# The first projection: rows of both operands 64 bytes apart mod 128, and two rows walked together

## The chip, the cores and the metric

The kernel runs on one core of one Trainium2 chip. The metric is device time in microseconds of one execution. The kernel before took 1110.11 us, the median of three runs (1110.0 to 1111.09). The profile is of one further execution, which took 1111.0 us, 1109.2 of them between its first and its last instruction.

## The reference, cut to what matters

One layer of a decoder for 256 tokens and 16 meta tokens, 2,048 wide. A normed input goes through the first projection, `w_in`, to 12,288 columns: queries, keys and values of 8 differential and 8 stick-breaking heads. Attention, the output projection and a squared-ReLU MLP follow.

```python
h = jnp.concatenate([dummy, meta, x], axis=1)
u = _rmsnorm(h, g_mix[l])
proj = jnp.einsum('bld,de->ble', u, w_in[l])          # the first projection
dq, dk, dv, sq, sk, sv = jnp.split(proj, split_at, axis=-1)
...                                                   # two kinds of attention -> mixed
h = h + jnp.einsum('ble,ed->bld', mixed, w_out[l])
m = _rmsnorm(h, g_mlp[l])
hid = jnp.square(jax.nn.relu(jnp.einsum('bld,df->blf', m, w_up[l])))
h = h + jnp.einsum('blf,fd->bld', hid, w_down[l])
```

## The kernel before

All large products are made of parts. A 32-bit operand is split into hi, its value rounded to the format in which TensorE (PE) takes it, and lo, the rest. Each product is then three matmuls into one sum: hi by hi, hi by lo, lo by hi.

The contraction over 2,048 is cut into 16 rows k of 128. For the first projection the moving operand is `u`: for each k one row of 272 tokens' hi and, right behind it, 272 tokens' lo (split_u, L165 to L171). A row is `ROW` = 576 floats long, 2,304 bytes, of which 2 x 272 are used. The stationary operand are the weights. They come in tiles of four rows k by 256 columns: the DMA brings one into `raw`, ScalarE (ACT) rounds it to `whi` (L175), VectorE (DVE) takes the difference, `wlo` (L177). A tile's four rows lie one behind the other, 1,024 bytes each. The first six tiles are split in two halves (rows 0 and 1, then 2 and 3), the later ones in one piece.

The stage has 24 strips of 256 columns, six kinds by four pairs of heads. Kinds 0 and 3, the queries, need the 256 tokens alone: their matmuls have 256 columns and begin 16 floats further in a row of `u`. The other four kinds have 272. A strip takes four weight tiles (c = 0 to 3), and each tile serves two halves j of 128 output columns, each summed in its own bank of PSUM. So a tile makes 2 x 4 x 3 = 24 matmuls, each with its own load of 128 by 128 weights (PEld in the profile). They are called in the loop over `units` behind `begin`: for each j, for each row kk of the tile, the three products (`products`, L966 to L978). L975 is hi by hi, L976 hi by lo, L977 lo by hi.

Where a weight tile's hi and lo begin is chosen in `offsets` (L244): each buffer is 64 floats longer than its data, and the data begin 0, 16 or 32 floats into it, that is 0 or 64 bytes mod 128. In the first projection lo is always 16 floats further than hi. The tiles for the output projection and the MLP take 0 or 16 for both. For the MLP's up products (L1060) it is 16 for the first tile of the first and third unit of a round, and 0 for the others.

The buffers of a kind are each 4,352 bytes long, 34 times 128, so they all begin at the same place mod 128. In the built program that is 32, and `u` begins at 96; `m`, the MLP's input, takes the same buffer as `u` later.

The order on each engine is written out by a planner (`Pace`): it keeps a model of the time on PE, DVE and ACT. The main loop issues the products; after each row it lets the planner issue whatever its model says is due: splits, loads, and the pieces of attention, whose matmuls fall between the products of the projection. `pc.stall` holds the model, not the chip, until the weights and the row of `u` are modelled as ready. The chip waits on semaphores. PE runs its queue in order.

Of the kernel before, what the change touches and what calls it, by code (L numbers as in the profile page):

```python
# [8 lines left out]
F32R = mybir.dt.float32r  # L9
# [4 lines left out]
P = 128  # L14
DM = 2048
SEQ = 256
META = 16
TOK = META + SEQ
KT = DM // P
EPS = 1e-6  # L20
NEG = -1e30
ROW = 576
LINE = 16
ROUNDS = 8
PAIRS = 4
# [97 lines left out]
def hymba_layer(ctx: ExitStack, tc: tile.TileContext, xT_d, xh_d, win_d, wout_d, wup_d, wdn_d, cst_d, par_d, out_d):  # L123
    nc = tc.nc
    cp = ctx.enter_context(tc.tile_pool(name="const", bufs=1))
    big = ctx.enter_context(tc.tile_pool(name="big", bufs=1))
# [8 lines left out]
    pc = Pace((("fetch", 9), ("weights", 9), ("once", 2), ("evac", 6), ("head", 4)))  # L135
# [23 lines left out]
    ident = cp.tile([P, P], F32, name="ident")  # L159
    xT = big.tile([P, KT, TOK], F32, tag="x", name="xT")  # L160
    big.tile([P, LINE], F32, name="pad_act")
    um = big.tile([P, KT, ROW], F32R, tag="act", name="u")[:, :, : 2 * TOK].rearrange("p k (a n) -> p k a n", a=2)
    big.tile([P, 3 * LINE], F32, name="pad_mix")
    mixed = big.tile([P, KT, 2, SEQ], F32R, tag="mix", name="mixed")

# [15 lines left out]
    strips = []  # L181
# [9 lines left out]
    order = [("in", *u) for u in dict.fromkeys(u[:2] for u in units)]  # L191
# [10 lines left out]
    for r in range(ROUNDS - 1):  # L202
        c = iter([key for i in range(PAIRS) for key in up(r + 1, i, range(4))])
# [37 lines left out]

    ring = {g: g - PARTS for g in range(len(order))}

    def offsets(g):  # L244

        what, *at = order[g]
        if what == "in":
            line = strips[at[0]][1] in (0, 3)
            return line * LINE, line * LINE + LINE
        line = at[1:] in ([0, 0], [2, 0]) if what == "up" else at != [0, 0] if what == "out" else True
        return line * LINE, line * LINE

    def part(g, pieces=1):
        if g < len(order) and g not in parts:
            pool, bufs, tag = wp, PARTS, "w"  # L260
            if g >= first_mlp:
                ring[g] = max(g - MLP_PARTS, first_mlp - PARTS + (g - first_mlp) % MLP_PARTS) if (g - first_mlp) % MLP_PARTS < PARTS else g - MLP_PARTS
                if (g - first_mlp) % MLP_PARTS >= PARTS:
                    pool, bufs, tag = mp, MLP_PARTS - PARTS, "v"
                    ring[g] = ring[g] if g - MLP_PARTS >= first_mlp else -1
            hi, lo = (
                pool.tile([P, 1024 + 4 * LINE], F32R, tag=tag + x, bufs=bufs, name=f"w{x}_{g}")[:, n : n + 1024]
                .rearrange("p (k n) -> p k n", k=4)
                for x, n in zip(("hi", "lo"), offsets(g))
            )  # L270
            parts[g] = (hi, lo)
            what, *at = order[g]
            fast = what in "ab" and (at[0], at[1]) in FAST
            pc.job("weights", (fast_a if what == "a" else fast_b)(g, hi, lo) if fast else halves(g, hi, lo, pieces))
# [46 lines left out]
    g = 0  # L321
    for c in range(4):
        n = 2 if c == 0 else 4
# [639 lines left out]
    def strip_start(s):  # L963
        return banks("acc", 2, f"acc_{s}")

    def products(s, out, j, k, kk, hi, lo):  # L966
        what, a, b = strips[s]
        cols = slice(P * j, P * j + P)
        h, l = hi[:, kk, cols], lo[:, kk, cols]
        first, last = k == 0, k == KT - 1  # L970
        if True:
            f, n = (META, SEQ) if a in (0, 3) else (0, TOK)
            xh, xl = um[:, k, 0, f : f + n], um[:, k, 1, f : f + n]
            o = out[j][:, :n]
            nc.tensor.matmul(o, lhsT=h, rhs=xh, start=first, stop=False)  # L975
            nc.tensor.matmul(o, lhsT=h, rhs=xl, start=False, stop=False)  # L976
            nc.tensor.matmul(o, lhsT=l, rhs=xh, start=False, stop=last)  # L977
            return pc.T(3 * (n / 2.4 + 2.5))  # L978
    seen_kinds = set()

    def finish(s, j, o, t):
        what, a, b = strips[s]
        if True:
            kind = "ds"[a // 3]
            gen = (diff_q, diff_k, None, stick_q, stick_k, None)[a]
            pc.job("evac", delayed(t, gen(b, j, o) if gen else values(kind, b, j, o)))
            seen_kinds.add((a, b, j))
            if a % 3 < 2 and {(a // 3 * 3, b, j), (a // 3 * 3 + 1, b, j)} <= seen_kinds:
                pc.job("head", (diff_head, stick_head)[a // 3](b, j))
# [43 lines left out]
    for s, c, kks in units:  # L1033
        g = index["in", s, c]
        if c == 0 and kks[0] == 0:
            open_strips[s] = strip_start(s)
        out = open_strips[s]
        if g >= seen:
            seen = g + 1
            begin(g, LEAD)  # L1040
        hi, lo = parts[g]
        for j in range(2):
            for kk in kks:
                k = 4 * c + kk
                pc.stall(("w", g, kk), ("u", k))
                t = products(s, out, j, k, kk, hi, lo)
                if k == KT - 1:
                    finish(s, j, out[j], t)
                pc.pump()
        if kks[-1] == 3:  # L1050
            done_at[g] = pc.pe

# [19 lines left out]
    for g in range(index["out", 0, 0], first_mlp):  # L1072
        _, u, c = order[g]
        if c == 0:
            out = banks("acc", 2, f"out_{u}")
            if u == 0:
                m = big.tile([P, KT, ROW], F32R, tag="act", name="m")[:, :, : 2 * SEQ].rearrange("p k (a n) -> p k a n", a=2)
        if u == 1 and c == 0:
            while pc.lanes["head"][0] or any(("mixed", k) not in pc.at for k in range(KT)):
                pc.pe += 100  # L1080
# [129 lines left out]
```

## Time and profile before

| what | before |
|---|---|
| median of three runs | 1110.11 us |
| the profiled execution | 1111.0 us |
| its span | 1109.2 us |
| PE busy | 1100.9 us, 99% |
| DVE busy | 945.1 us, 85% |
| ACT busy | 795.9 us, 72% |
| DMA read | 206.49 MB, 188 GB/s with the writes |
| granted PE clock | 1.00 |

An engine's busy time is the time in which at least one of its instructions runs. The matmuls of PE are pipelined: one is shown as some 280 ns long, and the next starts 110 to 130 ns behind it. So the length of a single row says little of PE's pace, and the sum of rows would be over 100%. The pace is the distance between starts, called a step here; it is read from the timeline, whose starts are given to 0.01 us, over many steps.

### The profile page before, as it was taken

How to read it: one execution, taken by the hardware profiler on the slowest of the kernel's cores; microseconds unless marked ns; L12 is line 12 of the kernel's file. 1: busy time of each engine (PE TensorE's matmuls, PEld its weight loads, DVE VectorE, ACT ScalarE, POOL GpSimd, SP SyncE). 2: the span in 40 equal slices, each digit the busy share in tenths (PEclk: the TensorE clock that was granted, in tenths of full speed). 3: DMA queues.
4: the chain of work that ended last, by engine and by line, in shares of the span. 5: the costliest groups of instructions: out<-in, count | busy, mean ns of one | idle time of the engine just before them, and what ended most of it. 6: DMA issues, size and time to landing. Idle time of an engine off the chain costs nothing.

```text
span 1109.2 us, 21822 instructions
## 1 busy us (share of the span) xinstructions
PE 1100.9 (99%) x8599; PEld 1057.5 (95%) x8599; DVE 945.1 (85%) x1459; ACT 795.9 (72%) x1283; POOL 1.1 (0%) x8
## 2 busy tenths in 40 slices
PE   8999999999999999999999999999999999999998
PEld 7999999999998888999999999999999999999987
DVE  6988988888877556689989989989989989989997
ACT  7878878878777555656677777777777677777663
POOL 0000000000000000000000000000000000000000
PEclk9999999999999999999999999999999999999999
DMA  8664544554544556545655655655655665655653
GB/s 326 188 228 144 158 135 138 169 158 143 166 159 149 191 179 221 189 154 191 227 191 191 225 192 192 224 194 191 222 192 195 219 196 193 219 194 196 213 183 137
DMA packets 58134, 210.00 MB, mean 189 GB/s; under 512 B 6576, under 2 KB 6832, under 8 KB 57904
## 3 DMA queue, kind: packets, MB, share of 16 engines
q1 hardware_dynamic: 58032, 208.61, 57.2%
q8 instruction: 67, 1.10, 0.4%
q14 instruction: 35, 0.29, 0.1%
HBM read 206.49 MB, written 2.10 MB: 188 GB/s over the span
## 4 chain that ended last, share of the span: by engine, by line
PE 98%; DVE 1%; DMA 1%; ACT 0%; SPq 0%; issue 0%; DVEq 0%
PE up L1060 32%; PE down L1066 28%; PE acc L975 9%; PE acc L977 8%; PE acc L976 8%; PE out L1066 8%; PE s_d L625 1%; DMA raw<-in_win 1%; PE po_s L665 1%; PE po_d L665 1%; PE z_s L625 1%; DVE wlo L177 0%; PE pt L829 0%; PE pq_dq L553 0%; SPq L228 0%; DVE H L899 0%
## 5 line engine op out<-in xcount | busy, mean ns | idle before, releaser
L177 DVE TENSOR_TENSOR wlo<-raw,whi 128x1024 fp32r<-128x1024 f32 (+2 forms) x478 | 538.8, 1158 | 104.0 <-ACT whi L175 102.5
L175 ACT CAST whi<-raw 128x1024 fp32r<-128x1024 f32 (+2 forms) x478 | 464.7, 997 | 200.6 <-PE up L1060 53.0
L1060 PE MATMUL up<-m,whi 128*128 128x256 f32 x2048 | 356.7, 277 | 0.0
L1066 PE MATMUL down<-whi,hid 128*128 128x256 f32 (+1 forms) x1552 | 313.1, 300 | 1.2 <-ACT down L927 1.2
L1060 PEld LDWEIGHTS up<-m,whi 128*128 128x128 f32 x2048 | 311.4, 188 | 1.9
L1060 PE MATMUL up<-m,wlo 128*128 128x256 f32 x1024 | 284.0, 277 | 0.0
L1066 PEld LDWEIGHTS down<-whi,hid 128*128 128x128 f32 x1552 | 244.1, 188 | 13.0 <-ACT down L927 1.4
L1066 PE MATMUL down<-wlo,hid 128*128 128x256 f32 (+1 forms) x776 | 233.3, 301 | 0.0
L975 PE MATMUL acc<-u,whi 128*128 128x272 f32 (+1 forms) x768 | 222.6, 290 | 1.2 <-ACT whi L175 1.2
L977 PE MATMUL acc<-u,wlo 128*128 128x272 f32 (+1 forms) x768 | 219.4, 286 | 0.7 <-DVE wlo L177 0.7
L976 PE MATMUL acc<-u,whi 128*128 128x272 f32 (+1 forms) x768 | 217.5, 283 | 0.0
L1060 PEld LDWEIGHTS up<-m,wlo 128*128 128x128 f32 x1024 | 192.8, 188 | 0.0
L1066 PEld LDWEIGHTS down<-wlo,hid 128*128 128x128 f32 x776 | 145.7, 188 | 6.3
L975 PEld LDWEIGHTS acc<-u,whi 128*128 128x128 f32 x768 | 144.5, 188 | 3.1 <-ACT whi L175 2.1
L977 PEld LDWEIGHTS acc<-u,wlo 128*128 128x128 f32 x768 | 144.3, 188 | 1.6 <-DVE wlo L177 1.5
L976 PEld LDWEIGHTS acc<-u,whi 128*128 128x128 f32 x768 | 144.5, 188 | 0.0
L1066 PE MATMUL out<-whi,mixed 128*128 128x512 f32 x256 | 80.3, 395 | 0.0
L290 DVE TENSOR_TENSOR raw<-raw 128x512 f32<-128x512 f32 x88 | 60.9, 692 | 3.0
L1066 PEld LDWEIGHTS out<-whi,mixed 128*128 128x128 f32 x256 | 47.3, 188 | 9.4
L1066 PE MATMUL out<-wlo,mixed 128*128 128x512 f32 x128 | 50.2, 392 | 0.0
L922 ACT COPY z<-down 128x512 f32<-128x512 f32 (+1 forms) x88 | 45.8, 528 | 2.9 <-PE down L1066 2.8
L871 ACT ACTIVATE hx<-up 128x512 f32<-128x512 f32 x32 | 19.1, 597 | 39.3 <-PE up L1060 39.3
(241 smaller groups left out, 918.5 us busy)
## 6 DMA issues: line engine op xcount, KB each, us to landing
raw<-in_wup SPq DMA_DIRECT2D x128, 512.0 KB, 4.7
raw<-in_wdn SPq DMA_DIRECT2D x128, 512.0 KB, 3.9
raw<-in_win SPq DMA_DIRECT2D x95, 512.0 KB, 3.7
raw<-in_wout SPq DMA_DIRECT2D x32, 512.0 KB, 3.5
H<-in_xh SPq DMA_DIRECT2D x1, 2048.0 KB, 8.4
out<-H SPq DMA_DIRECT2D x8, 256.0 KB, 2.0
xT<-in_x SPq DMA_DIRECT2D x3, 544.0 KB, 9.7
cst<-in_cst SPq DMA_DIRECT2D x1, 609.0 KB, 11.8
```

What stands on the lines that cost most here:

```text
L175: nc.scalar.copy(hi, src)
L177: nc.vector.tensor_tensor(lo, src, as32(hi), op=ALU.subtract)
L290: nc.vector.tensor_tensor(raw[:, 3::-3], first, raw[:, 3:1:-1], op=ALU.add)
L625: nc.tensor.matmul(dst, lhsT=q[x][rows, cols], rhs=k[y][rows, :n], start=i == 0, stop=i == 2)
L665: nc.tensor.matmul(o, lhsT=l, rhs=r, start=i == 0, stop=i == len(todo) - 1)
L871: nc.scalar.activation(x[:, 0:4].rearrange("p a b -> p (a b)"), o, AF.Relu)
L922: nc.scalar.copy(Z[u][:, at], o[i][:, :n])
L975: nc.tensor.matmul(o, lhsT=h, rhs=xh, start=first, stop=False)
L976: nc.tensor.matmul(o, lhsT=h, rhs=xl, start=False, stop=False)
L977: nc.tensor.matmul(o, lhsT=l, rhs=xh, start=False, stop=last)
L1060: nc.tensor.matmul(out, lhsT=w[a], rhs=x[:, b], start=first and i == 0, stop=last and i == 2, skip_group_check=True)
L1066: nc.tensor.matmul(out, lhsT=x[a], rhs=w[b], start=first and i == 0, stop=last and i == 2, skip_group_check=check)
```

## The change

The row of `u` grows from 576 to 592 floats. Its two halves, hi and lo, are now 296 floats each instead of 272, so hi begins at 0 and lo 1,184 bytes further, and neighbouring rows k are 2,368 bytes apart: 64 mod 128. A first-projection weight tile uses its whole buffer: four rows of 272 floats, of which the last 256 hold data, so neighbouring rows are 1,088 bytes apart, 64 mod 128 as well. Hi and lo begin alike. `m` keeps its place but packs its rows without a gap.

The walk changes too. For kinds of 272 columns two neighbouring rows are taken together: hi by hi of both, hi by lo of both, lo by hi of both. For kinds of 256 columns a row's three products stay together, but a tile is walked by even rows for j = 0 and 1, and then by odd rows for j = 1 and 0. The planner is let in after two rows instead of one. All products are now called from one line, L976.

```diff
-ROW = 576
+ROW = 592
...
-    um = big.tile([P, KT, ROW], F32R, tag="act", name="u")[:, :, : 2 * TOK].rearrange("p k (a n) -> p k a n", a=2)
+    um = big.tile([P, KT, ROW], F32R, tag="act", name="u").rearrange("p k (a n) -> p k a n", a=2)
...
-            hi, lo = (
-                pool.tile([P, 1024 + 4 * LINE], F32R, tag=tag + x, bufs=bufs, name=f"w{x}_{g}")[:, n : n + 1024]
-                .rearrange("p (k n) -> p k n", k=4)
-                for x, n in zip(("hi", "lo"), offsets(g))
-            )
+            whole = [pool.tile([P, 1024 + 4 * LINE], F32R, tag=tag + x, bufs=bufs, name=f"w{x}_{g}") for x in ("hi", "lo")]
+            if order[g][0] == "in":
+                hi, lo = (x.rearrange("p (k n) -> p k n", k=4)[:, :, LINE:] for x in whole)
+            else:
+                n = offset(g)
+                hi, lo = (x[:, n : n + 1024].rearrange("p (k n) -> p k n", k=4) for x in whole)
...
+        f, n = (META, SEQ) if a in (0, 3) else (0, TOK)
+        todo = [(kk, i) for i in range(3) for kk in kks] if n == TOK else [(kk, i) for kk in kks for i in range(3)]
+        for kk, i in todo:
+            k = 4 * c + kk
+            nc.tensor.matmul(
+                out[j][:, :n], lhsT=(hi, hi, lo)[i][:, kk, cols], rhs=um[:, k, i % 2, f : f + n],
+                start=k == 0 and i == 0, stop=k == KT - 1 and i == 2,
+            )
...
-        for j in range(2):
-            for kk in kks:
-                k = 4 * c + kk
-                pc.stall(("w", g, kk), ("u", k))
-                t = products(s, out, j, k, kk, hi, lo)
-                if k == KT - 1:
-                    finish(s, j, out[j], t)
-                pc.pump()
+        if strips[s][1] in (0, 3):
+            todo = [(j, [kk for kk in kks if kk % 2 == odd]) for odd in range(2) for j in (range(2), (1, 0))[odd]]
+        else:
+            todo = [(j, kks[n : n + 2]) for j in range(2) for n in range(0, len(kks), 2)]
+        for j, some in todo:
+            pc.stall(*[("w", g, kk) for kk in some], *[("u", 4 * c + kk) for kk in some])
+            t = products(s, out, c, j, some, hi, lo)
+            if 4 * c + some[-1] == KT - 1:
+                finish(s, j, out[j], t)
+            pc.pump()
...
-                m = big.tile([P, KT, ROW], F32R, tag="act", name="m")[:, :, : 2 * SEQ].rearrange("p k (a n) -> p k a n", a=2)
+                m = big.tile([P, KT * ROW], F32R, tag="act", name="m")[:, : KT * 2 * SEQ].rearrange("p (k a n) -> p k a n", k=KT, a=2)
```

On PE, in a strip of 272 columns, the last row of a weight tile and the first of the next stand like this before (`acc` is the sum in PSUM, one for each output half, `whi` and `wlo` the weights, and u the moving operand; each row is one matmul):

```order
L975 MATMUL acc_1_1919<-u,whi_1808 128x272
L976 MATMUL acc_1_1919<-u,whi_1808 128x272
L977 MATMUL acc_1_1919<-u,wlo_1809 128x272
L975 MATMUL acc_0_1918<-u,whi_1852 128x272
L976 MATMUL acc_0_1918<-u,whi_1852 128x272
L977 MATMUL acc_0_1918<-u,wlo_1853 128x272
```

The same engine in the changed program, also in a strip of 272 columns: the last two rows of a tile for the one output half, the last two for the other, and the attention scores (`z`) behind them (x4 are four matmuls of one text: hi by hi of two rows, then hi by lo of both):

```order
L976 MATMUL acc_0_3526<-u,whi_3438 128x272 x4
L976 MATMUL acc_0_3526<-u,wlo_3439 128x272 x2
L976 MATMUL acc_1_3527<-u,whi_3438 128x272 x4
L976 MATMUL acc_1_3527<-u,wlo_3439 128x272 x2
L623 MATMUL z_s_3559<-kh_s_3382,qh_s_3519 128x144
L623 MATMUL z_s_3559<-kl_s_3383,qh_s_3519 128x144
```

The three products of a row no longer stand together: six matmuls of two rows do, and neighbouring matmuls have weights of different rows.

On PE, in a strip of 256 columns, the last row of one output half and the first of the other stand like this before:

```order
L975 MATMUL acc_0_2153<-u,whi_2114 128x256
L976 MATMUL acc_0_2153<-u,whi_2114 128x256
L977 MATMUL acc_0_2153<-u,wlo_2115 128x256
L975 MATMUL acc_1_2154<-u,whi_2114 128x256
L976 MATMUL acc_1_2154<-u,whi_2114 128x256
L977 MATMUL acc_1_2154<-u,wlo_2115 128x256
```

In the changed program this is the end of one weight tile of such a strip and the start of the next, with the two matmuls of a head's norm (`pn`) between them:

```order
L976 MATMUL acc_0_2110<-u,whi_2051 128x256 x2
L976 MATMUL acc_0_2110<-u,wlo_2052 128x256
L358 MATMUL pn_s_2210<-oh_s_2163,ones 128x256
L359 MATMUL pn_s_2210<-ol_s_2164,ones 128x256
L976 MATMUL acc_0_2110<-u,whi_2112 128x256 x2
L976 MATMUL acc_0_2110<-u,wlo_2113 128x256
```

A row's three products still stand together, but the tile ends with the output half with which it began, and the next begins with that half again, so the pieces of attention fall between other rows. Before the last product of the stage PE had 439 matmuls of attention in 81 places; now it has 432 in 78.

## Rows read from the trace of the kernel before

**Rows 1.** the page: span, busy time by engine, the chain that ended last
```profile
span 1109.2 us, 21822 instructions
...
PE 1100.9 (99%) x8599; PEld 1057.5 (95%) x8599; DVE 945.1 (85%) x1459; ACT 795.9 (72%) x1283; POOL 1.1 (0%) x8
...
PE 98%; DVE 1%; DMA 1%; ACT 0%; SPq 0%; issue 0%; DVEq 0%
PE up L1060 32%; PE down L1066 28%; PE acc L975 9%; PE acc L977 8%; PE acc L976 8%; PE out L1066 8%; PE s_d L625 1%; DMA raw<-in_win 1%; PE po_s L665 1%; PE po_d L665 1%; PE z_s L625 1%; DVE wlo L177 0%; PE pt L829 0%; PE pq_dq L553 0%; SPq L228 0%; DVE H L899 0%
```

**Rows 2.** stretch: length, busy us of PE, PEld, DVE, ACT, POOL, clock, DMA
```profile
120.00:160.00 40.00, 40.00 (x336) 39.05 (x336) 36.49 (x84) 31.71 (x78) 0.00 (x0) 1.00 0.51 157
...
sum 280.00, PE 279.88 PEld 277.00 DVE 241.61 ACT 226.14 POOL 0.00; mean PE 39.98 PEld 39.57 DVE 34.52 ACT 32.31 POOL 0.00
```

**Rows 3.** PE groups, 5.5 to 338.3 us: count | busy us, mean ns | idle us
```profile
L975 PE MATMUL acc<-u,whi 128*128 128x272 f32 x512 | 149.9, 293 | 0.0
...
L975 PE MATMUL acc<-u,whi 128*128 128x256 f32 x256 | 72.6, 284 | 1.2 <-ACT whi L175 1.2
L977 PE MATMUL acc<-u,wlo 128*128 128x256 f32 x256 | 72.2, 282 | 0.7 <-DVE wlo L177 0.7
```

**Rows 4.** timeline, PE: start us, us, engine, line, operands, shape; 272 columns
```profile
165.35 0.29 PE L975 MATMUL acc<-u,whi 128*128 128x272 f32 x1
165.47 0.28 PE L976 MATMUL acc<-u,whi 128*128 128x272 f32 x1
...
172.01 0.29 PE L975 MATMUL acc<-u,whi 128*128 128x272 f32 x1
```

**Rows 5.** timeline, PE, a run of 256 columns
```profile
187.89 0.28 PE L976 MATMUL acc<-u,whi 128*128 128x256 f32 x1
...
193.66 0.28 PE L977 MATMUL acc<-u,wlo 128*128 128x256 f32 x1
```

**Rows 6.** timeline, PE, the MLP's up products (x2: two starts, one row)
```profile
455.51 0.40 PE L1060 MATMUL up<-m,whi 128*128 128x256 f32 x2
...
457.67 0.40 PE L1060 MATMUL up<-m,whi 128*128 128x256 f32 x2
...
458.03 0.39 PE L1060 MATMUL up<-m,whi 128*128 128x256 f32 x2
...
459.05 0.39 PE L1060 MATMUL up<-m,whi 128*128 128x256 f32 x2
```

**Rows 7.** groups by line and shape, DVE and ACT, splits into hi and lo
```profile
L177 DVE TENSOR_TENSOR wlo<-raw,whi 128x1024 fp32r<-128x1024 f32 x378 | 452.0, 1221 | 101.0 <-ACT whi L175 99.8 <-PE down L1066 0.3
...
L891 DVE TENSOR_TENSOR hid<-hx,hid 128x1024 fp32r<-128x1024 f32 x32 | 39.0, 1219 | 0.3 <-ACT hid L889 0.2
...
L175 ACT CAST whi<-raw 128x1024 fp32r<-128x1024 f32 x378 | 388.5, 1048 | 182.8 <-PE up L1060 50.4 <-PE down L1066 37.3 <-DVE raw L294 36.5
...
L889 ACT CAST hid<-hx 128x1024 fp32r<-128x1024 f32 x32 | 33.5, 1048 | 2.7 <-DVE hx L883 2.7
```

**Rows 8.** timeline, PE, the start, with waits in brackets
```profile
5.59 0.39 PE L975 MATMUL acc<-u,whi 128*128 128x256 f32 x1 [0.83 <-ACT whi L175]
...
6.32 0.39 PE L977 MATMUL acc<-u,wlo 128*128 128x256 f32 x1 [0.22 <-DVE wlo L177]
...
8.18 0.38 PE L975 MATMUL acc<-u,whi 128*128 128x256 f32 x1 [0.41 <-ACT whi L175]
```

**Rows 9.** timeline, PE, up products around four transposes
```profile
436.35 0.39 PE L1060 MATMUL up<-m,whi 128*128 128x256 f32 x2
...
438.05 0.39 PE L1060 MATMUL up<-m,whi 128*128 128x256 f32 x2
...
438.74 0.60 PE L829 MATMUL pt<-ident,H 128*128 128x128 f32 x4
...
439.53 0.40 PE L1060 MATMUL up<-m,whi 128*128 128x256 f32 x2
...
441.30 0.40 PE L1060 MATMUL up<-m,whi 128*128 128x256 f32 x2
```

More of the change, by code (lines that the diff above doesn't have):

```diff
@@ L242, in hymba_layer, with offset @@
     ring = {g: g - PARTS for g in range(len(order))}
-    def offsets(g):
+    def offset(g):
         what, *at = order[g]
-        if what == "in":
-            line = strips[at[0]][1] in (0, 3)
-            return line * LINE, line * LINE + LINE
         line = at[1:] in ([0, 0], [2, 0]) if what == "up" else at != [0, 0] if what == "out" else True
-        return line * LINE, line * LINE
+        return line * LINE
     def part(g, pieces=1):
@@ L964, in strip_start, with products @@
         return banks("acc", 2, f"acc_{s}")
-    def products(s, out, j, k, kk, hi, lo):
+    def products(s, out, c, j, kks, hi, lo):
         what, a, b = strips[s]
         cols = slice(P * j, P * j + P)
[L969 to L978, printed above, removed]
+        f, n = (META, SEQ) if a in (0, 3) else (0, TOK)
[6 more added lines that the diff above has]
+            )
+        return pc.T(3 * len(kks) * (n / 2.4 + 2.5))
     seen_kinds = set()
```

## The prediction

> **What bounds the kernel now.** I read the page first. TensorE (PE) is busy 99% of the span, VectorE (DVE) 85%, ScalarE (ACT) 72%, and the chain of waits that ended last is 98% PE; 25% of it is the three product lines of the first projection, L975 to L977 [rows 1]. So the change works on the engine that sets the end, and a nanosecond saved per product there is a nanosecond of the span unless another engine becomes late. Next the stretches: from 40 to 320 us PE idles 0.12 us of 280, at the full granted clock (1.00, the 2.4 GHz level), while DVE is busy 241.61 us, or 86%, with 36.49 of 40 in the tightest stretch [rows 2]. There is nothing to win from waits, only from the step between the starts of two neighbouring products. The groups by shape give the counts: three lines of 512 products with 272 columns, three of 256 with 256 columns, so 1,536 and 768 [rows 3]; their only waits are 1.2 and 0.7 us, all at the start.
>
> The busy times of a group overlap (a product is shown as 0.29 us long, the next starts 0.12 us behind it [rows 4]), so I take steps from the timeline. 272 columns: starts at 165.35 and 172.01, 54 steps apart, 123.3 ns each [rows 4]. 256 columns: 187.89 to 193.66, 49 steps, 117.8 ns [rows 5]. The same 256 columns in the MLP's up products: 455.51 to 457.67, 18 steps of 120.0 ns, and right behind it 458.03 to 459.05, 9 steps of 113.3 ns [rows 6]. Same engine, clock, shape and kind of operand: three levels, 113, 118 and 120.
>
> What differs between the last two is the weights' place. In the built program the moving operand of the up products begins 96 bytes into a 128-byte line in both; the stationary one begins at 96 in the slow group (`line` is 1 for that weight tile) and at 32 in the other. Both operands are read by PE at once: the load of the next weights goes on while the present product streams. So 64 bytes apart is good, the same half line costs 6.7 ns a step.
>
> The Trainium skill, "TensorE: Matmul & The Clock Gate", section "Step-by-step: what each phase is for", says the opposite: the two operands come through independent read ports, and loading the next weights takes no read bandwidth from the running product. By that rule places would not matter and the sum would be zero; the trace disagrees, with 120.0 against 113.3 ns.
>
> **What the first projection does now.** Worked out from the layout, (stationary, moving) bytes mod 128 run, for 272 columns, (32, 96), (32, 32), (96, 96), over and over, and the 256-column kinds have the same with every number moved by 64. The next weights are always 64 away from the present stream, as in the good up group. But the stream jumps: a 272-column row is 1,088 bytes, so it ends 64 further than it began; (32, 96) runs on seamlessly into (32, 32), that one into (96, 96), and then the third breaks. With 256 columns two of the three steps break. So I read 123.3 and 117.8 as a good level plus breaks. The good level for 256 columns is 113.3; for 272 I scale it by columns, 113.3 x 272/256 = 120.4. The poor level for 272 is likewise 117.8 x 272/256 = 125.2.
>
> **The change part by part.** It adds and removes no product: 2,304 before and after.
>
> 1. 272 columns (16 of the 24 strips). Two rows are walked together, hi-hi, hi-lo, lo-hi: (96, 96), (32, 32), (96, 0), (32, 64), (96, 96), (32, 32). The hi-lo rows stand 32 off, since a half of a 592-float row is 1,184 bytes, 32 mod 128. Three of the six steps (inside hi-hi, inside lo-hi, and on to the next pair) are now seamless with the next weights 64 away: 120.4. The other three touch a hi-lo product: into it the stream jumps by 32, inside it the next weights are 32 away, out of it both. No row of before shows operands 32 apart in this stage; the bounds are the good and the same-half level, 120.4 and 120.0 x 272/256 = 127.5. I take the middle between the good and the poor level, 122.8, since 32 is half of the 64 that a break has now. Mean (120.4 + 122.8)/2 = 121.6, a gain of 1.7 ns x 1,536 = 2.6 us (bounds: 2.9 x 1,536 = 4.5 us, and with 127.5 for the three a mean of 124.0, a loss of 1.0 us).
>
> 2. 256 columns (8 strips). Even rows first for both halves, then odd rows, so the stationary place stays, and the moving one runs 32, 64, 32, with the weights at 96 (odd rows: 64 further). One step in three is exactly like the good up group, 113.3. The two that touch the shifted row lie between 113.3 and 120.0; by the same choice I take 115.6, the middle between 113.3 and 117.8. Mean 114.8, gain 3.0 x 768 = 2.3 us (bounds 4.5 x 768 = 3.5 us, and none, with 120.0 for the two).
>
> 3. The splitting into hi and lo writes four pieces of 256 with gaps instead of one run of 1,024 for these 96 weight tiles. Cost nothing: hid is written in gapped pieces of 128 already, and takes 1,219 ns on DVE against 1,221 in one run, 1,048 against 1,048 on ACT [rows 7].
>
> 4. The wider row moves all later tiles by 1,024 bytes, a multiple of 128, and m packs its rows 2,048 instead of 2,304 bytes apart, also multiples; the output and MLP products keep their places mod 128. Cost nothing, save that a level can be inherited (below).
>
> 5. Start-up. The even-odd walk asks for rows 2 and 3 of a weight tile after three products instead of six. In the first 12 us PE already waits for splits 0.83, 0.22 and 0.41 us [rows 8], and tiles arrive in two halves there. I add 0.2 us, with 0 and 1.5 us (four such tiles by 0.4) as ends: what waits earlier there waits less later, since the same loads and splits end the chain.
>
> 6. Cover. PE would be through with the stage some 5 us sooner in 330, 1.5%; DVE at 86% goes to 87.5%, and its tightest stretch from 91 to 93%. I cost this at nothing; if that cover were gone, ACT's and DVE's queue of attention pieces would make PE wait, and what is won is the most that could be lost.
>
> Sum: 2.6 + 2.3 - 0.2 = 4.7 us. The profiled execution took 1111.0 us (span 1109.2 and 1.8 around it), so 1106.3; the median of the runs is 0.9 below that execution, so 1105.4.
>
> **Rivals.**
> - All steps go to the good level, because a 32-byte jump breaks nothing: 2.9 x 1,536 + 4.5 x 768 = 4.5 + 3.5, less 0.2, 7.8 us: 1102.3. For it: up products hold 113.3 over long runs. Against: nothing shows a 32-byte offset to be free.
> - The level is inherited, not set by places. After four transposes at 438.74 the up products, same line, same shape, same places, go from 113.3 (436.35 to 438.05, 15 steps) to 118.0 (439.53 to 441.30, 15 steps) [rows 9], and stay there until the 120 ns group; behind that they are at 113.3 again [rows 6]. The first projection is cut by attention products some 80 times, so each piece may draw either level whatever the walk is: (120.4 + 125.2)/2 = 122.8 and (113.3 + 117.8)/2 = 115.6 would still gain 0.8 + 1.7 = 2.5 us, all poor levels would lose 1.9 x 1,536 = 2.9 us, and a mix of them nothing. I put this case at 1110, from 1108 to 1112.
> - The other side: the hi-lo products collide, and the stream comes out of it at the poor level. Three of six 272-column steps at 127.5 and the others at 125.2 give 126.4, a loss of 3.1 x 1,536 = 4.8 us; two of three 256-column steps at 120.0 and one at 117.8 give 119.3, a loss of 1.5 x 768 = 1.2 us; with the start's 0.2, 6.2 us: 1116.3. It decides once the three steps behind a collision don't recover; if they do, the loss is 1.0 + 0.2 and the time 1111.3. For it: same-half reads cost 6.7 ns without fail, and now even the seamless step in three of the 256-column kinds leaves the mean at 117.8. Against: 32 apart is not the same place, and behind the 120 ns group the stream recovered at once [rows 6].
>
> - Places don't matter in this stage: the 123.3 and 117.8 come from something else in it, such as the splits' traffic, and stay. The start's 0.2 us alone is left: 1110.3. Against it speak the 6.7 ns between the up groups, where the same kind of split runs beside the products [rows 6]. This is the time by the Trainium skill's rule of independent ports, quoted above.
>
> **How the numbers follow.** Forecast 0.37, all good 0.21, inherited 0.21, collision 0.16, no effect of places 0.05. A measurement of this kernel can tell about 0.2% (2.2 us) from no change, so faster means under 1107.9 and slower over 1112.3. Faster: most of the first two and a little of the third, 0.58; same: most of the third, the last, the forecast's weak end and the collision that recovers, 0.28; slower: the collision that doesn't, and the start's 1.5 us on top of no gain, 0.14. The range runs from all good with 1 us to spare, 1101.0, to the edge of slower, 1112.3, and leaves most of the lasting collision out; the forecast's own is 1103 to 1108.
>
> **What would show it.** Right: in the timeline, runs of 272-column products at 121 to 122.5 ns a step and of 256-column ones at 114 to 116; the up products at 113.3 and 118.0 where they are now; the output products unchanged; the first projection's end about 5 us earlier; gapped splits still 1.22 and 1.05 us. Wrong: steps of 123 and 118 as before (inherited or no effect), of 126 or more around the hi-lo products (collision), or new PE waits for L175 and L177 behind the first 12 us.

## The result, and the profile after

The changed kernel took 1121.16 us (median of 4 runs, 1120.24 to 1122.65) where the kernel before took 1110.35 on the same chip: a ratio of 1.0096, 95% interval 1.0084 to 1.0108. I had predicted 1105.4 with a range to 1112.3. The forecast had the wrong sign, and the time is outside the range.

The page of the changed kernel (span, busy time, the chain that ended last), which answers to [rows 1]:

```profile
span 1120.9 us, 21807 instructions
...
PE 1108.3 (99%) x8599; PEld 1064.0 (95%) x8599; DVE 945.5 (84%) x1459; ACT 794.9 (71%) x1283; POOL 1.1 (0%) x8
...
PE 95%; DVE 2%; ACT 1%; DMA 1%; issue 0%; SPq 0%; DVEq 0%; ACTq 0%
```

The same 8,599 products, still 99% busy; DVE and ACT have not a microsecond more to do. But the chain's PE share fell from 98% to 95%: somewhere PE now waits. To see where, cut both traces at the same four places: the first projection, the output projection, the MLP up to its last up product, and the rest. Before (stretch: length, busy us of PE, PEld, DVE, ACT, POOL, clock, DMA):

```profile
5.60:338.30 332.70, 331.45 (x2750) 327.11 (x2751) 284.18 (x590) 269.50 (x591) 0.00 (x0) 1.00 0.55 175
338.30:431.80 93.50, 93.50 (x435) 77.18 (x434) 55.92 (x71) 49.24 (x79) 0.00 (x0) 1.00 0.55 180
431.80:1058.30 626.50, 626.50 (x5160) 612.72 (x5159) 560.75 (x731) 448.95 (x577) 0.00 (x0) 1.00 0.61 200
1058.30:1109.20 50.90, 45.85 (x252) 39.31 (x250) 42.86 (x66) 25.23 (x33) 0.00 (x0) 1.00 0.48 166
```

and after:

```profile
5.60:340.90 335.30, 334.02 (x2746) 330.72 (x2747) 281.70 (x584) 264.81 (x580) 0.00 (x0) 1.00 0.53 174
340.90:440.40 99.50, 96.01 (x439) 78.70 (x438) 58.68 (x78) 52.99 (x89) 0.00 (x0) 0.98 0.49 169
440.40:1067.00 626.60, 626.60 (x5161) 612.75 (x5160) 559.29 (x730) 448.14 (x577) 0.00 (x0) 1.00 0.60 200
1067.00:1120.90 53.90, 47.65 (x252) 40.59 (x250) 44.51 (x67) 25.92 (x34) 0.00 (x0) 0.96 0.47 156
```

The 11.7 us between the two spans split into 2.6 in the first projection, 6.0 in the output projection, 0.1 in the MLP and 3.0 at the end. The largest part lies in a stage whose products and places the change doesn't touch. Also, the output projection's stretch holds 78 DVE instructions instead of 71, and 89 of ACT instead of 79: pieces of attention that stood in the first projection before.

The waits of PE in the changed kernel (us in total, times, longest):

```profile
PE out L1071 <- ACT mixed L175: 3.5, 1, 3.5
PE down L1071 <- ACT down L925: 1.9, 1, 1.9
...
PE s_d L623 <- DVE kl_d L177: 0.5, 1, 0.5
...
PE pq_dq L551 <- DVE sq_dk L525: 0.4, 1, 0.4
PE pv_d L600 <- DVE vt_d L593: 0.4, 1, 0.4
```

The first is new, the second was 1.2 before. The last three are new too; they lie in the first projection, at 57, 119 and 59 us. The timeline of PE, and of ACT and DVE, around the first of them:

```profile
363.38 0.28 PE L359 MATMUL pn_s<-ol_s,ones 128*128 128x256 f32 x1
367.15 0.96 PE L1071 MATMUL out<-whi,mixed 128*128 128x512 f32 x2 [3.49 <-ACT mixed L175]
...
365.04 0.42 ACT L366 ACTIVATE oa_s<-os_s 128x256 f32<-128x256 f32 x1
366.70 0.40 ACT L175 CAST mixed<-oa_s 128x256 fp32r<-128x256 f32 x1 [1.24 <-DVE oa_s L790]
...
366.24 0.42 DVE L790 SCALAR_TENSOR_TENSOR oa_s<-oa_s,o_s 128x256 f32<-128x256 f32 x1
```

PE does the last norm sum of the last head (`pn_s`) at 363.38, and its very next product needs the row of `mixed` that comes out of that sum: through ACT, DVE and ACT again, until 367. In the kernel before the last such write of `mixed` began at 358.62 on ACT, and nobody waited. Behind the wait the clock falls (PE alone):

```profile
367.00:368.00 1.00, 0.85 (x3) 1.00 0.83 319
368.00:369.00 1.00, 1.00 (x6) 0.89 0.34 123
369.00:370.00 1.00, 1.00 (x4) 0.50 0.00 0
...
371.00:372.00 1.00, 1.00 (x4) 0.50 0.00 0
372.00:373.00 1.00, 1.00 (x6) 0.90 0.00 0
```

A granted clock of 0.50 is the 1.2 GHz level. There a product of 512 columns steps 0.427 us instead of 0.229. Added up by their starts, the stage's 384 output products take 90.9 us instead of 88.9. So its 6.0 us are 3.5 of waiting, 2.1 of slower products, and 0.4 for four attention matmuls that stood in the first projection before. The same happens once more at the end: 1.9 us of waiting at 1078, and the clock at 0.50 from 1079 to 1082.

Now the steps in the first projection, which answer to [rows 4] (272 columns, 58 steps) and [rows 5] (256 columns, 53 steps):

```profile
177.23 0.41 PE L976 MATMUL acc<-u,wlo 128*128 128x272 f32 x2
...
184.47 0.41 PE L976 MATMUL acc<-u,whi 128*128 128x272 f32 x2
...
189.75 0.40 PE L976 MATMUL acc<-u,whi 128*128 128x256 f32 x2
...
196.02 0.28 PE L976 MATMUL acc<-u,wlo 128*128 128x256 f32 x1
```

7.24/58 = 125 ns and 6.27/53 = 118.3 ns. Over all uninterrupted steps of the stage the means are 125.2 and 118.2, against 123.7 and 117.7 before: 1.5 x 1,536 + 0.5 x 768 = 2.7 us. I had forecast 121.6 and 114.8. The stage as a whole is 2.6 us longer: beside the steps it has some 1.2 us of new waits, and four attention matmuls fewer.

### The profile page after: what moved, and what is told of

It is laid out like the page before. It is cut to its first block, busy times and chain, and to the rows that moved or that the text cites. A ratio compares the mean times of both kernels' runs of the same rounds, so it can differ in the third digit from the quotient of the medians.

```text
span 1120.9 us, 21807 instructions
## 1 busy us (share of the span) xinstructions
PE 1108.3 (99%) x8599; PEld 1064.0 (95%) x8599; DVE 945.5 (84%) x1459; ACT 794.9 (71%) x1283; POOL 1.1 (0%) x8
## 4 chain that ended last, share of the span: by engine, by line
PE 95%; DVE 2%; ACT 1%; DMA 1%; issue 0%; SPq 0%; DVEq 0%; ACTq 0%
PE up L1065 30%; PE down L1071 27%; PE acc L976 25%; PE out L1071 8%; DVE wlo L177 1%; DMA raw<-in_wup 1%; ACT whi L175 1%; PE po_d L663 1%; PE po_s L663 1%; PE s_d L623 1%; PE z_s L623 1%; PE pt L827 0%; PE pq_dq L551 0%; DMA xT<-in_x 0%; DVE H L897 0%
## 5 line engine op out<-in xcount | busy, mean ns | idle before, releaser
L177 DVE TENSOR_TENSOR wlo<-raw,whi 128x1024 fp32r<-128x1024 f32 (+2 forms) x478 | 538.7, 1157 | 104.3 <-ACT whi L175 102.7
L175 ACT CAST whi<-raw 128x1024 fp32r<-128x1024 f32 (+2 forms) x478 | 464.2, 997 | 211.8 <-PE up L1065 52.1
L976 PE MATMUL acc<-u,whi 128*128 128x272 f32 (+1 forms) x1536 | 267.7, 290 | 0.4 <-ACT whi L175 0.4
L976 PEld LDWEIGHTS acc<-u,whi 128*128 128x128 f32 x1536 | 223.7, 190 | 2.4 <-ACT whi L175 1.3
L976 PE MATMUL acc<-u,wlo 128*128 128x272 f32 (+1 forms) x768 | 179.1, 287 | 0.0
L976 PEld LDWEIGHTS acc<-u,wlo 128*128 128x128 f32 x768 | 129.4, 189 | 0.2 <-DVE wlo L177 0.2
L925 ACT COPY down<-z 128x512 f32<-128x512 f32 (+1 forms) x76 | 40.9, 538 | 2.4
L292 DVE TENSOR_TENSOR raw<-raw 128x256 f32<-128x256 f32 x88 | 37.4, 425 | 3.0
```

Of the source, the lines that this page charges most:

```text
L175: nc.scalar.copy(hi, src)
L177: nc.vector.tensor_tensor(lo, src, as32(hi), op=ALU.subtract)
L292: nc.vector.tensor_tensor(raw[:, 1], raw[:, 2], raw[:, 1], op=ALU.add)
L925: nc.scalar.copy(new[i][:, :n], Z[u2][:, at])
L976: nc.tensor.matmul(out[j][:, :n], lhsT=(hi, hi, lo)[i][:, kk, cols], rhs=um[:, k, i % 2, f : f + n], start=k == 0 and i == 0, stop=k == KT ...
```

## The experiments

All edits are against the changed kernel unless said otherwise. The kernel before stood at 1110.3 to 1110.5 in each set.

**1. The places undone, walk and order kept.** Rows of `u` and of the weights stand as in the kernel before; the two-row walk and the planner's turns are those of the change.

```diff
-ROW = 592
+ROW = 576
-hi, lo = (x.rearrange("p (k n) -> p k n", k=4)[:, :, LINE:] for x in whole)
+first = (strips[order[g][1]][1] in (0, 3)) * LINE
+hi, lo = (x[:, n : n + 1024].rearrange(...) for x, n in zip(whole, (first, first + LINE)))
```

> The changed kernel's walk and its order on every engine, with the rows of both operands where they lay before (rows of u 576 floats, lo 64 bytes behind hi in the weights, tile rows without gaps). Theory A (most of the loss is the order: the last heads of attention are issued later, the output projection waits for them, and PE's clock falls behind that wait): the wait for the last mixed row in front of the output projection's first unit stays at about 3.5 us, the stage behind it at half clock for about 4 us, together 6 us; steps of the first projection as they come, so 1115 to 1120 us. Theory B (the loss is where the rows lie): the steps go back to 123.3 and 117.8 and the time to 1110 to 1111 us.

Measured: 1118.86 us, ratio 1.0077 (1.0064 to 1.0089). The wait of 3.5 us for `mixed` is there, and half the clock behind it; the output projection's stretch is 100.6 us long. So most of the loss has nothing to do with where rows lie. The 272-column steps are 124.8 here, with the old places: the walk alone takes them off the 123.7.

**2. The planner's turns undone, places and two-row walk kept.** The planner is let in after every 3 products, as before, and not after the products of a whole two-row step; the halves are walked one after the other, so that the order of attention among the products is that of the kernel before. (In the two traces each attention matmul stands behind the same number of products.)

```diff
+            done += 1
+            if done % 3 == 0:
+                yield pc.T(3 * (n / 2.4 + 2.5))
-        return pc.T(3 * len(kks) * (n / 2.4 + 2.5))
...
-    todo = [(j, [...]) for odd in range(2) for j in (range(2), (1, 0))[odd]]
+    todo = [(j, [...]) for j in range(2) for odd in range(2)]
```

> The changed kernel's places and its walk of two rows (256-column kinds: even rows, then odd ones, for each output half in turn), but the planner is let in after each three products, as before, so that the order on all engines outside the first projection's own products is that of before. Theory A: no wait in front of the output projection and none of the half clock there; only the first projection's steps cost, 2.6 us as in the changed kernel, so 1112.5 to 1113.5 us. Theory B: 1118 to 1121 us, as the changed kernel.

Measured: 1113.13 us, ratio 1.0022 (1.0013 to 1.0031). PE's waits behind the start are gone, but for the 1.2 us at the end that the kernel before has too; the output projection takes 93.40 us at full clock:

```profile
341.10:434.50 93.40, 93.40 (x434) 77.19 (x433) 55.75 (x71) 49.09 (x78) 0.00 (x0) 1.00 0.55 180
```

This splits the loss: 8.0 us (1121.16 - 1113.13) go with the order, 2.8 with the steps, which stay at 125.2 and 118.4 here. The profiled runs of the two kernels differ by 8.9 us: 6.1 in the output projection and 3.0 at the end, while the first projection takes 335.3 us in the one and 335.5 in the other.

**3. No 32-byte offset anywhere.** As run 2, with the low part of `u` at 1,152 bytes into its row (0 mod 128), so that hi-lo products have the same places as the others.

```diff
+SEAM = 288
-um = big.tile(..., name="u").rearrange("p k (a n) -> p k a n", a=2)
+um = big.tile(..., name="u")[:, :, : 2 * SEAM].rearrange("p k (a n) -> p k a n", a=2)
```

> As the run before it, but lo begins 1,152 bytes behind hi in a row of u (0 mod 128) instead of 1,184 (32 mod 128), so that all steps inside a strip are seamless with the next weights 64 bytes away. If the 32-byte shift holds the steps at the poor level (theory C): 272 columns go to 120 to 121 ns, 256 columns to 113 to 115 ns, and the time to 1102 to 1105 us. If a level is inherited from what ran before and these places do not set it (theory D): 125 and 118 ns, 1112 to 1114 us.

Measured: 1113.1 us, ratio 1.0025 (1.0016 to 1.0034): as run 2. Steps of 125.8 (272 columns) and 117.5 (256). With every step free of the 32-byte jump that I had priced as half a break, nothing is won. The theory that a seamless stream is good falls.

**4. The kernel before, with the planner let in after every second row.**

```diff
-                pc.pump()
+                if kk % 2:
+                    pc.pump()
```

> The kernel before with one edit: the planner is let in after every second row instead of every row. Places and walk are those of before. Theory A: the pieces of the last heads move back by 3 to 27 products of the output projection (those of the changed kernel by up to 42), so steps stay at 123.3 and 117.8 and the output projection waits little or nothing: 1109 to 1112 us. If letting the planner in half as often is harmful in itself (theory E): a wait of over 2 us in front of the output projection and 1114 us or more.

Measured: 1116.31 us, ratio 1.0053 (1.004 to 1.0065), steps as before. Letting the planner in half as often costs by itself, without any other edit, but not always in the same place. Here, in the profiled run, PE loses most at the start, where a weight tile's split comes late, and little at `mixed`:

```profile
PE acc L977 <- DVE wlo L177: 3.6, 5, 2.2
...
PE out L1067 <- DVE mixed L177: 0.8, 1, 0.8
```

I had expected 1109 to 1112 of the theory that I held; it was wrong on what this edit costs. The time is that of the other theory, but the wait of over 2 us that it put in front of the output projection came at the start.

**5. The disputed step by itself.** Behind the last instruction of the kernel before, 30 series of bare products with every place chosen, DVE and ACT idle.

```diff
+for i, test in enumerate(tests):       # e.g. S * 24 + A * 48, (A * 3 + B * 3) * 6
+    for k, (n, (w, x)) in enumerate(test):
+        nc.tensor.matmul(out[:, :n], lhsT=probe[:, w : w + P], rhs=probe[:, x : x + n], ...)
+    nc.vector.tensor_scalar(probe[:, :2048], out[:, :1]..., op0=ALU.min, op1=ALU.max)
```

> The kernel before, and behind its last instruction 30 short series of bare products (1,080 of them, 256 or 272 columns; operands lie in one tile, no output uses them; the last series' values go nowhere), each behind a wait of TensorE for VectorE. Written as (place of the stationary, place of the moving operand) mod 128. Theory D (the step is carried over from what TensorE did before): 24 products at (32, 96) directly behind a wait step at 117.5 to 118.5 ns, and the same 48 behind 24 products at (96, 96) at 113 to 114; two transposes in the midst of such a series take it back to 117.5 to 118.5. Theory P (the two places alone decide, as the prediction's steps 1 and 2 had it): the same step for (32, 96) in all of these, and for three products at (32, 96) in turn with three at (96, 32) 114.5 to 115.5, whatever went before. Theory N (the splits that VectorE and ScalarE write beside the first projection raise the step): here, with both engines idle, every series of 256 columns at opposite places steps below 115, behind a wait too. For 272 columns D expects one kind of series to differ by over 3 ns with what stood before it; P expects (32, 32) in turn with (96, 96) at 120 to 122; N expects all at 120 or below. The time itself: about 150 us above the kernel before.

Measured (1368.22 us in all, 258 above the kernel before and not 150: there are 1,222 products, not the 1,080 that I had counted, the 29 waits between the series add up to 69 us, and 18 series ran in part or whole at half the clock). Rows of the timeline of PE: the first two are stretches of one series, in which three products at (96, 96) are followed by 21 at (32, 96), twice over; the third is a run at (96, 96); the last two are 272 columns at (96, 96) and at (32, 96). A row's length is that of its steps and of one product, 0.27 to 0.29:

```profile
1216.92 2.55 PE L1175 MATMUL probe<-probe 128*128 128x256 f32 x21
...
1219.19 2.28 PE L1175 MATMUL probe<-probe 128*128 128x256 f32 x18
...
1182.64 2.31 PE L1175 MATMUL probe<-probe 128*128 128x256 f32 x18
...
1236.37 2.95 PE L1175 MATMUL probe<-probe 128*128 128x272 f32 x22
...
1280.87 2.88 PE L1175 MATMUL probe<-probe 128*128 128x272 f32 x22
```

That is 113.5, 118, 120.0, 126.7 and 123.3 ns a step. Same places, same three products ahead, and yet 113 the first time and 118 the second. (Ahead of the three stood a wait the first time, and 21 products at (32, 96) the second.) Behind 24, 12, 6, 3 and 1 products at (96, 96), a run at (32, 96) went on at 113.3, 117.7, 113.3, 117.8 and 113.3. In the two at 117.7 and 117.8 the clock had risen from half in the midst of the run; but the two stretches above differ just so at full clock throughout. A run at (96, 32) directly behind a wait stepped at 113.3, and one behind 24 at (96, 96) at 117.8. The series that put 24 at (32, 96) directly behind a wait ran at half the clock to its end and says nothing. Two transposes in the midst of a good run left it good. Three in turn with three at (96, 32): 117.2 in the mean. So theory P (the places decide) falls, and theory N with it: DVE and ACT are idle and 117.8 is still there. Theory D is right that a level, once entered, stays for the run, and wrong on what sets it: neither products in the same half nor transposes switch it reliably. The same half of the line steps at 120.0 with everything else at rest. By the rule of independent ports in the Trainium skill, "TensorE: Matmul & The Clock Gate", section "Step-by-step: what each phase is for", it would not matter where the two operands lie; the trace goes on disagreeing, with 120.0 against 113.3 and 117.8.

For 272 columns none of the 15 series, where it ran at full clock, stepped below 123.3 in the mean; (32, 32) in turn with (96, 96), the pattern that was to be good, came to 123.3 once and 125.0 the other time. None of them holds the good level of 120.4, which I had scaled from 256 columns.

**6. The places alone, walked row by row, order as before.**

```diff
-todo = [(kk, i) for i in range(3) for kk in kks] if n == TOK else [(kk, i) for kk in kks for i in range(3)]
+todo = [(kk, i) for kk in kks for i in range(3)]
...
+todo = [(j, [kk]) for j in range(2) for kk in kks]
```

> The change's places alone: rows of both operands as the change lays them, but walked row by row (hi hi, hi lo, lo hi of one row, then the next) with the planner let in after each row, in the order of the kernel before. Theory A (the order that the planner makes costs some 8 us, the steps some 2.8): without the planner's part it comes out at 1110 to 1114, no wait of over 1.5 us ahead of the output projection. Within that, theory D (which step holds is carried over from what went before, places do not set it): 272 columns at 124.5 to 126, 256 at 117.5 to 118.5, time 1112 to 1114. Theory P (the places with row by row walking are as good as those of before): 272 columns at 123 to 124, time 1110 to 1111. Were the new places themselves what delays the output projection, it would be above 1117.

Measured: 1111.82 us, ratio 1.0016 (1.0006 to 1.0025), the output projection at full clock. 272 columns step at 124.8, 256 at 118.2. So the places alone cost 1.5 us, and don't delay the output projection.

**7 and 8. The planner's turns undone only near the end of the stage**: in the last 4 of the 24 strips, and in the last 12.

```diff
+            if s >= len(strips) - 4 and done % 3 == 0:      # 12 in the second kernel
+                yield pc.T(3 * (n / 2.4 + 2.5))
```

> The change as it is, but in the last 4 of the 24 strips of the first projection the planner is let in after every 3 products, not after the products of a whole step. Theory A (what is lost is the lateness of the last heads alone): their last piece is now written behind 60 products of the output projection, before it stood behind 84, the row of mixed that is needed by about the 90th is there in time; no wait of over 1 us in the output projection, no stretch of half the clock, and 1112.5 to 1115 (the kernel before plus some 2.8 for the steps). Theory B (the lateness is piled up over all strips, or what comes late is something else in the stage): 1117 to 1121 with the wait of about 3.5 us still there.

> As the run before the last, but in the last 12 of the 24 strips: the last piece of the last heads then stands behind 42 products of the output projection, as in the kernel before (60 with 4 strips, 84 in the change). Theory A' (the lateness of the last heads, which piles up over the second half of the strips, makes the wait and the clock's fall): no wait of over 1 us ahead of a product of the output projection, no stretch at half the clock there, the output projection in 93 to 93.6 us as before (99.8 in the change), and 1112.5 to 1115 with what the first 12 strips and the steps cost. Theory B' (it is set already in the first half, or the position among the instructions does not decide): the wait stays at 1 us or more, and 1116 to 1120.

Measured: 1118.92 us (1.0071, 1.0057 to 1.0085) with 4 strips, 1114.52 (1.0035, 1.0022 to 1.0049) with 12. With 4 strips the wait is shorter, in two parts, and the clock falls all the same:

```profile
366.04 0.50 PE L1076 MATMUL out<-whi,mixed 128*128 128x512 f32 x1 [1.21 <-ACT mixed L175]
367.33 0.50 PE L1076 MATMUL out<-whi,mixed 128*128 128x512 f32 x1 [0.79 <-DVE mixed L177]
...
369.00:370.00 1.00, 1.00 (x4) 0.50 0.71 283
```

With 12 strips both are gone, and the stretch, cut as above, is 93.40 us again:

```profile
341.60:435.00 93.40, 93.40 (x434) 77.10 (x433) 55.29 (x69) 49.00 (x77) 0.00 (x0) 1.00 0.56 180
```

| kernel | last piece of the last head stands behind | waits for `mixed` in the profiled run | first output product to first up product |
|---|---|---|---|
| before | 42 output products | none | 93.5 us |
| last 12 strips undone | 42 | none | 93.5 |
| last 4 strips undone | 60 | 1.21 + 0.79 us | 97.3 |
| run 4 | 69 | 0.8 us | 95.1 |
| changed, and run 1 | 84 | 3.5 us | 99.6 and 100.6 |

The second column is counted in the order of PE's products. Run 4 waits less with 69 than the kernel with 60, and its clock stays at 1.00 there: the last piece's place in the order is not all that sets the wait. With 4 strips neither theory was right as written: lateness is piled up over more than those. With 12 the wait goes, as theory A' had it, while 1114.52 is still 1.4 us above run 2. In the profiled run PE has the waits of 0.5, 0.4 and 0.4 us in the first half of the strips, which run 2 doesn't have. They are of that size, but the intervals of the two ratios overlap, so that they make up the difference is not shown.

**9. The kernel before, with long runs of one pair of places** in the 256-column strips from the third on, each behind four products in the same half.

```diff
-return line * LINE, line * LINE + LINE
+return line * LINE, line * LINE + (0 if line and at[0] > 1 else LINE)
...
+for at, (i, kk) in enumerate((i, kk) for i in (1, 0, 2) for kk in kks):
```

> The kernel before with one edit, in the 256-column strips from the third on: stationary rows all at 96 mod 128, and of four rows first the 4 products with the low part of u (at 96, the same half), then the other 8 (at 32, opposite): long runs of one pair of places, in front of each a few products in the same half. The planner is let in after every 3 products as before. From the probe: same half 120.0, opposite either 113.3 or 117.8, which of the two is taken on entering and then kept. Theory D: if each entry took the good level, 512 products gain 4.4 and 256 lose up to 2.3 of 117.7: the 256-column steps at 115.5 in the mean, 1.7 us gained, 1108.4 to 1109.2; if it is even chances, 117 and 1109.5 to 1110.5; if always the poor one, 118.5 and 1110.5 to 1111.5. Theory P (places alone, both at the levels of the probe's best): only the first of these.

Measured: 1110.32 us, ratio 0.9999 (0.999 to 1.0008), 256-column steps at 117.8 in the mean against 117.7. No version of the steps was found that beats the kernel before.

## Why the prediction was wrong

**Reading the bound: right, and half of the matter.** PE sets the end, and the steps in the first projection were what the change was about. But "there is nothing to win from waits" was read from a stage in which nothing waited; that there was something to lose from them I didn't ask.

**Part 6, cover: this is the step that failed by most.** I looked for lateness only as DVE and ACT becoming busier, "I cost this at nothing", and bounded the loss by what the steps would win. Yet the change also halves the planner's turns: 6 products between two of them instead of 3. A head is a chain of pieces, each of which is placed once the planner thinks that the one before it is through; with fewer turns each link goes out later. The order of the instructions, which was to be had before the run, shows it: 432 attention products inside the first projection instead of 439, and the last norm sum behind 84 output products instead of 42. The row that it feeds is needed by the very next of them, the 85th. That was worth 8.0 us (run 2), which no term of my sum held. In the profiled runs it shows as 3.5 us of waiting, 2.1 of products at half the clock and 0.4 of moved attention matmuls in the output projection, and as 3.0 us at the end, of which it is open whether the order makes them (below). In the first projection itself the order costs nothing that can be told from run 2. The bound "what is won is the most that could be lost" was no bound, since it came from another mechanism.

**What differs is the weights' place (the reading behind parts 1 and 2): wrong.** I had two neighbouring groups at 120.0 and 113.3 with different places, and took the places for the cause of all three levels. The 120.0 of the same half stood up in run 5. The 113.3 and 117.8 are both had with one and the same pair. The trace of before held the case against me, and I had quoted it as a rival: 113.3 before four transposes and 118.0 after, with no change of place [rows 9]. It was given 0.21 where it deserved the most.

**Part 1, 272 columns:** forecast 121.6, measured 125.2. It failed at the scaling of 113.3 to 120.4: of 15 series of 272 columns none came below 123.3 (run 5). It failed at the breaks as well: with every step seamless the mean was 125.8 (run 3). The kernel before, at 123.7, was already near the best that was seen. Places cost here and walk costs here: 124.8 with the new places alone (run 6), 124.8 with the new walk alone (run 1).

**Part 2, 256 columns:** forecast 114.8, measured 118.2. It failed at the claim that one step in three "is exactly like the good up group". With every step inside a group of six alike (run 3) the mean was 117.5, with long runs of one pair (run 9) 117.8.

**Parts 3 and 4: right.** The gapped splits cost nothing, and the MLP takes 626.6 us against 626.5. The rows that answer to [rows 7]:

```profile
L177 DVE TENSOR_TENSOR wlo<-raw,whi 128x1024 fp32r<-128x1024 f32 x378 | 452.0, 1220 | 101.8 <-ACT whi L175 100.4 <-PE down L1071 0.3
L175 ACT CAST whi<-raw 128x1024 fp32r<-128x1024 f32 x378 | 388.3, 1047 | 196.2 <-PE up L1065 49.5 <-PE down L1071 41.3 <-DVE raw L292 34.8
```

**Part 5, the start:** the first projection's first product is at 5.65 us against 5.59, and the waits for its splits are shorter than before, 0.4 us against 1.9. But in the profiled run that is not the walk's doing alone: the first two dozen products step at 0.213 us, the length that 256 columns had at half the clock in run 5 (the profile lists 1.00 there, without a record of the clock before 10.4 us), and a slower PE waits less for its splits. Between these two rows lie three steps:

```profile
8.04 0.63 PE L976 MATMUL acc<-u,whi 128*128 128x256 f32 x2
...
8.68 0.63 PE L976 MATMUL acc<-u,whi 128*128 128x256 f32 x2
```

At 13.9 us both kernels have begun about as many products, 51 and 50, so the start costs nothing here; what the walk alone would cost isn't shown.

**The rivals.** The poor levels throughout, 125.2 and 117.8 with a loss of 2.9 us, which I had as one end of the inherited case, are what the steps did: 125.2 and 118.2, a loss of 2.7 us, and 2.8 by run 2. "The hi-lo products collide" gave 1116.3, on the right side, by a mechanism that run 3 refutes: without the 32-byte offset the time is the same. "Places don't matter" (1110.3) is nearest in spirit for 256 columns, and not right for 272, where both places and walk move the mean by 1 ns. The sign "new PE waits for L175 and L177 behind the first 12 us", listed as what would show me wrong, is the one that came: 0.5 us for L177 at 57 us in this stage, and the 3.5 us for L175 in the one behind.

**Still open.** What picks 113.3 or 117.8 when a run is entered. What beside its place in the order sets how long PE waits for the last row of `mixed`. And the 3.0 us at the end: in the profiled run a wait for ACT grew from 1.2 to 1.9 us, one of 0.4 for DVE is new, and the clock fell behind the first. Run 1, with the same order, has 1.2 us there and no such loss; the spans of the other three runs of the changed kernel are 1.2 to 2.4 us shorter, so it may be in part a matter of the single execution.

## What to carry to other kernels

Where a planner places side work between products, the number of its turns is part of the schedule: an edit that groups products must keep its turns, or be priced by where the last link of each chain comes to stand in the instruction order and by who needs it. A difference between two groups of rows that differ in place is not yet an effect of place: first look for the same place at two levels. And a level measured for one shape is not scaled to another by its columns without a row of that shape.

## What the runs showed of the hardware

- A short wait of PE can cost up to about its own length again. Behind 3.49 us, 1.93 us and 1.21 + 0.79 us of idle time the granted clock stood at 0.50 for 3 to 4 us, and behind the same 3.49 us in run 1 for nearly 7, with 512-column products at 0.427 us instead of 0.229 (256 columns: 0.213 instead of 0.113 to 0.120, run 5). It doesn't always come. Of the 29 waits of 2.4 us between the series of run 5, 17 were followed by a stretch at half the clock and 12 were not. In run 4 PE waited 2.24 us at 18 us and the clock stayed at 1.00; behind the 1.2 us at the end of the kernel before it stayed there too.
- Products of 256 columns run at 113.3, 117.8 or 120.0 ns a step, in long constant runs. 120.0 goes (run 5) with both operands in the same half of a 128-byte line; between the other two the same places were seen at both, with all other engines idle.
